# One 512-column value projection at the end of units 1 and 2, in place of two of 256 columns

## The chip, the cores and the metric

The kernel runs on one core of a Trainium2 chip. The metric is device microseconds of one execution; the figure for a kernel is the median of its runs. Times inside an execution are counted from the start of the profiler's span. TensorE is PE in the rows (its weight loads PEld), VectorE is DVE, ScalarE is ACT, and the DMA queue is SyncE's, SP.

## The reference, cut to what matters

```python
hn = rmsnorm(h_res, norm_w) * (1 + scale) + shift
proj = hn @ w_in
dq, dk, dv, dg, gq, gk, gv, gg, glr = split(proj, IN_OFFSETS)
a_out = diff_attention(rope(dq), rope(dk), dv, lam)
a_out = rmsnorm(a_out, diff_norm_w) * (1 - lam_init) * silu(dg)
b_out = gla_chunk_causal(gq, gk, gv, log_a)
b_out = rmsnorm(b_out, gla_norm_w) * silu(gg)
mixed = concat([a_out, b_out]) @ w_out
out = rmsnorm(h_res + gate * mixed, final_norm_w)
```

There are 1024 tokens of width 2048. `dv` holds the values of 8 softmax heads (128 columns each) and `gv` those of 4 gated linear heads (256 columns each). The change touches only how these two are projected for some of the heads.

## The kernel before

**Halves and units.** Tokens go in two halves of 512. In each half, four units g = 0 to 3 follow each other; unit g does the softmax heads 2g and 2g+1 and the linear head g. Everything is carried as a pair of reduced-precision parts (high and low), so each product is three matmuls. TensorE is shared by all of it, and each engine runs its own list of instructions strictly in the order that the compiler's scheduler wrote; it need not be the order of the source.

**A unit, in the order of the source** (`unit`, L821 to L885): projections `dk`, `dq`, `dg` of the first head, the narrow slab `dv` of the unit (L846), attention of the first head, `dk`, `dq`, `dg` and attention of the second, `gq`, two gate projections `gg`, the narrow slab `gv` (L873), and the linear head (`gla`, L773 to L817). The scheduler runs attention and `gla` of one unit among the projections of the same and the next unit. In unit 0 of the first half the projections were made earlier, and its linear head runs late, during unit 1.

**Two kinds of projection.** `proj_b` (L194) makes one tile of 128 features by 512 tokens: 48 matmuls with 512 columns moving. `proj_a` (L204) makes a slab with tokens on the partitions: for 256 columns 192 matmuls with 256 columns moving, 16 input blocks by 4 token blocks by 3. Its results are two PSUM tiles `pa_0` and `pa_1`, each with two token blocks.

**Weights.** Each piece is 128x1024 (`wload`, L168): one DMA into one of two raw buffers `wr`, then a high part by ScalarE (L179) and a low part by VectorE (L180) into one of three buffers `w`. A piece can be converted only when TensorE has done with the piece three before it.

**PSUM.** All projections take their tiles in turn from one pool of four banks (`pj`, L109). A tile's next user waits until the last reader of the bank has finished. At a unit's end the turn is `dg` of the second head, `gq`, first `gg`, second `gg`, and then the slab: a narrow slab takes the banks of `dg` and `gq`; a slab of four tiles would also take those of the two `gg`.

**What frees these banks.** `gq` is read by L836 and L837, which write the one buffer `gq`; they wait for the last matmul of the unit before's linear head (`o`, L804), which reads that buffer. The first `gg` bank is free after `silu_gate` has copied it (L242) into the one buffer `gg`; that copy waits until the unit before has used its `gg` up: the linear head's output is normalized, transposed by TensorE (`to`, L815), multiplied by the gate (L816), and split and stored, for j = 0 and 1, through one buffer `wr2` (`mix_out`, L731): the second split waits for the first store to land.

**Leaving PSUM.** `split` (L228) is a ScalarE cast and a VectorE subtraction from the same bank. `gv` leaves in two pairs of 128x512 (L882), `dv` in four of 128x256 (L612). In the first half the values `vb` take two of three `vb` buffers, `gv` the third and the one buffer `ka`; the buffer `va` is not used until the half's end.

**Side work.** In the first half, units 1 and 2, a list `later` (norm rows, L953, for the second half, and the first rows of the gate, L906) is spread among the weight loads: each row is a 256 KB load to a two-part buffer `stage`, one or two VectorE operations, and for the norm rows a store. At the end of unit 3, `second_hn` (L957) loads 8 pairs of input blocks back through the buffers `ka`, `va`, `kb` in turn and splits them into `hn` for the second half.

Of the kernel before, what the change touches and what calls it, by code (L numbers as in the profile page):

```python
# [10 lines left out]
F32 = mybir.dt.float32  # L11
F32R = mybir.dt.float32r
# [7 lines left out]
P = 128  # L20
# [24 lines left out]
OFF = dict(dq=0, dk=1024, dv=2048, dg=3072, gq=4096, gk=4608, gv=5120, gg=6144, glr=7168)  # L45
# [8 lines left out]
B_AT = {c: i for i, c in enumerate(B_CHUNKS)}  # L54

A_SLABS = [(n, g) for g in range(4) for n in ("dv", "gv")] + [("gk", 1)]
A_AT = {c: i for i, c in enumerate(A_SLABS)}


def lay_out(inputs):  # L60
    f = lambda a: np.ascontiguousarray(np.asarray(a))
    x = f(inputs["x"])[0]
    w = f(inputs["w_in"])[0].reshape(KT, P, -1)
    out = {}
    out["x"] = f(x)
    out["xt"] = f(x.reshape(2, TOK, KT, P).transpose(0, 3, 2, 1))
    out["ct"] = f(inputs["c"]).reshape(KT, P).T.copy()
    ada = f(inputs["w_ada"])[0].reshape(8, 2, P, 3, 8, 256)
    out["wada"] = f(ada[:, :, :, 1::-1].transpose(4, 0, 2, 1, 3, 5)).reshape(8, 8, P, 2, 512)
    out["wada0"] = f(out["wada"][0].reshape(8, P, 2, 2, 2, P).transpose(4, 0, 2, 1, 3, 5).reshape(2, 4, 4, P, 256).transpose(0, 1, 3, 2, 4))  # L70
    out["wgate"] = f(ada[:, :, :, 2].reshape(KT, P, 4, 512).transpose(2, 0, 1, 3))
    out["winb"] = f(np.stack([w[:, :, OFF[n] + i * P:OFF[n] + (i + 1) * P] for n, i in B_CHUNKS]).transpose(0, 2, 1, 3))
    out["wina"] = f(np.stack([w[:, :, OFF[n] + i * 256:OFF[n] + (i + 1) * 256] for n, i in A_SLABS]).transpose(0, 2, 1, 3))
    out["wing"] = f(np.concatenate([w[:, :, OFF["gk"]:OFF["gk"] + 256], w[:, :, OFF["glr"]:OFF["glr"] + 16]], axis=2).transpose(1, 0, 2))
    out["wout"] = f(f(inputs["w_out"])[0].reshape(KT, P, 4, 512).transpose(2, 1, 0, 3))
    out["nw"] = f(f(inputs["norm_w"])[0].reshape(KT, P).T)
    b = f(inputs["b_ada"])[0]
    out["bss"] = f(b[:2 * D].reshape(2, KT, P).transpose(2, 0, 1))
    out["bg"] = f(b[2 * D:].reshape(1, D))
    out["lam"] = f(np.stack([f(inputs[n])[0] for n in ("lambda_q1", "lambda_q2", "lambda_k1", "lambda_k2")]).reshape(1, 256))  # L80
    out["dnw"] = f(f(inputs["diff_norm_w"])[0].reshape(P, 1))
    out["gw2"] = f(inputs["gla_gate_w2"])[0].copy()
    out["gb"] = f(inputs["gla_gate_b"])[0].reshape(1, 512).copy()
    out["gnw"] = f(f(inputs["gla_norm_w"])[0].reshape(2, P).T)
    out["fw"] = f(inputs["final_norm_w"]).reshape(1, D).copy()
    inv = (np.float32(10000.0) ** (-np.arange(0, 64, 2, dtype=np.float32) / np.float32(64))).astype(np.float32)
    ang = (np.arange(S, dtype=np.float32)[None, :] * inv[:, None]).astype(np.float32)
    cos, sin = np.cos(ang).astype(np.float32), np.sin(ang).astype(np.float32)
    out["rope"] = f(np.stack([np.concatenate([cos] * 4), np.concatenate([-sin, sin, -sin, sin])], axis=1))
    j = np.arange(P)  # L90
    out["ltri"] = f(((j[:, None] // CHUNK == j[None, :] // CHUNK) & (j[:, None] > j[None, :])).astype(np.float32))
    out["ind"] = f((j[:, None] // CHUNK == np.arange(2)[None, :]).astype(np.float32))
    return out


def body(ctx, tc, A, out):
    nc = tc.nc
# [18 lines left out]
    vs_d = [dram.tile([P, 4, 2, P], F32, name=f"vsd{h}", tag=f"vsd{h}") for h in range(HEADS)]  # L116
# [70 lines left out]
    hn = [None] * KT  # L187
# [16 lines left out]
    def proj_a(src, act, n=256, kpp=4, per_bank=2):  # L204
        nb = 4 // per_bank
        pss = [pj_p.tile([P, TOK], F32, name=f"pa{w_n[0]}_{b}", tag="pj") for b in range(nb)]
        for k0 in range(0, KT, kpp):
            kn = min(kpp, KT - k0)
            w = wload(src[:, k0:k0 + kn, :], kn * n)
            for t in range(4):  # L210
                ps = pss[t // per_bank]
                o = ps[:, (t % per_bank) * n:(t % per_bank) * n + n]
                for kk in range(kn):
                    kt = k0 + kk
                    ah, al = act[kt][:, 0, t * P:(t + 1) * P], act[kt][:, 1, t * P:(t + 1) * P]
                    wh, wl = w[:, 0, kk * n:(kk + 1) * n], w[:, 1, kk * n:(kk + 1) * n]
                    st = kt == 0 and t % per_bank == 0
                    PE.matmul(o, ah, wh, start=st, stop=False, skip_group_check=True)  # L218
                    PE.matmul(o, ah, wl, start=False, stop=False, skip_group_check=True)  # L219
                    PE.matmul(o, al, wh, start=False, stop=kt == KT - 1, skip_group_check=True)  # L220
        return pss
# [6 lines left out]
    def split(hi, lo, src, lo_eng=None):  # L228
        SC.copy(hi, src)
        (lo_eng or V).tensor_tensor(lo, src, hi.bitcast(F32), ALU.subtract)  # L230
# [58 lines left out]
    for c in range(N_FIRST):  # L289
        n, i = B_CHUNKS[c]  # L290
# [149 lines left out]
    pss = st_tiles(0, 4, "b")  # L440
# [164 lines left out]
    def make_v(pss, half, g):  # L605
        vt = [hd_p.tile([P, 4, 2, P], F32R, name=f"vb{half}_{2 * g + i}", tag="vb", bufs=3) for i in range(2)]
        for b in range(2):
            v4 = pss[b].rearrange("p (t h d) -> p t h d", t=2, h=2)
            for i in range(2):
                hi, lo = vt[i][:, 2 * b:2 * b + 2, 0, :], vt[i][:, 2 * b:2 * b + 2, 1, :]  # L610
                with tc.high_priority(offset=EVAC):
                    split(hi, lo, v4[:, :, i, :])  # L612
        if half == 0:
            for i in range(2):
                nc.sync.dma_start(vs_d[2 * g + i], vt[i].bitcast(F32))
        return vt
# [200 lines left out]
            mix_out(gg[:, j, :], wr2, half, 8 + 2 * g + j)  # L817

    QS = P ** -0.5

    def unit(half, g, first, kdec):  # L821

# [20 lines left out]
        kb0 = make_k(src("dk", h0), half, h0)  # L843
        qt0 = make_q(src("dq", h0), half, h0)
        g0 = gate_tile(h0)
        vt = make_v(dv_ps if first else proj_a(A["wina"][A_AT[("dv", g)]], hn), half, g)  # L846
        attention(half, h0, qt0, kb0, vt[0], g0)
        kb1 = make_k(src("dk", h1), half, h1)
        qt1 = make_q(src("dq", h1), half, h1)
# [19 lines left out]
            tmp = misc.tile([P, 2, TOK], F32, name=f"ggt{half}{g}{j}", tag="rt", bufs=2)  # L869
            silu_gate(gg[:, j, :], s_, gnw[:, j:j + 1], tmp)  # L870
        swap = half == 0 and g == GHEADS - 1
        if not first:
            pss = proj_a(A["wina"][A_AT[("gv", g)]], hn)  # L873
        if swap:
            second_hn()
        spare_ka = half == 0 and not swap
        gv = [hd_p.tile([P, 4, 256], F32R, name=f"gv{half}{g}{i}", tag="ka" if spare_ka and i else "vb",
                        bufs=None if spare_ka and i else 3) for i in range(2)]
        for b in range(2):
            ts = slice(2 * b, 2 * b + 2)  # L880
            with tc.high_priority(offset=EVAC):
                split(gv[0][:, ts, :], gv[1][:, ts, :], gv_acc[:, ts, :] if first else pss[b].rearrange("p (t c) -> p t c", t=2))  # L882
# [225 lines left out]
```

## Time and profile before

| | us |
|---|---|
| median of 3 runs (1954.07 to 1956.4) | 1954.24 |
| the profiled execution, its own time | 1955.52 |
| its span, first to last instruction | 1953.7 |
| PE busy in the span | 1905.5 (98%) |
| DVE busy in the span | 1321.9 (68%) |
| ACT busy in the span | 968.7 (50%) |
| PE's part of the chain that ended last | 86% |

The profiled execution lies 1.3 us above the median, and its span 1.8 us below its own time. Busy time of PE runs from a matmul's start to its end, and neighbours overlap, so the step from one start to the next is what a matmul takes of the engine. Idle time is named with the instruction behind it and what released it.

In the first half the narrow slabs lie, by the timeline of PE, at 301.9 to 326.2 (`dv` of unit 1), 401.2 to 430.3 (`gv` of unit 1), 469.8 to 497.9 (`dv` of unit 2), 577.7 to 611.5 (`gv` of unit 2), 651.7 to 677.8 (`dv` of unit 3) and 753.8 to 779.2 (`gv` of unit 3).

### The profile page before, as it was taken

What the parts mean: (1) busy time and instruction counts of PE and PEld (TensorE: products, weight loads), DVE (VectorE), ACT (ScalarE), POOL (GpSimd) and SP (SyncE); (2) the same over time, 40 slices, a digit from 0 to 9 for tenths busy, and PEclk for the clock granted to TensorE, in tenths of its full rate; (3) what the DMA queues carried; (4) which work ended last, traced back from release to release, by engine and by line L of the source; (5) the groups of instructions that cost most, each with busy time, mean ns of one, the idle gap of its engine ahead of it and who ended that gap; (6) DMA issues with size and microseconds to landing.
All of it is one profiled execution on the core that took longest, in us unless ns stands there. A gap on an engine that the chain in (4) does not pass through costs nothing.

```text
span 1953.7 us, 28965 instructions
## 1 busy us (share of the span) xinstructions
PE 1905.5 (98%) x11118; PEld 1677.0 (86%) x11118; DVE 1321.9 (68%) x2496; ACT 968.7 (50%) x1811; POOL 0.7 (0%) x6
## 2 busy tenths in 40 slices
PE   7999999999989999999999999999999999899998
PEld 4888999899868989889899898989888998688888
DVE  7897876577779767656676666866785675534444
ACT  4222865566545566545545555554654544323323
POOL 0000000000000000000000000000000000000000
PEclk9899999999999999999999999999999999799999
DMA  9884434332665444433344323533263723466543
GB/s 362 294 290 136 155 125 141 119 106 87 209 210 166 136 138 150 135 89 101 97 154 117 106 91 108 162 111 99 87 198 117 267 86 106 167 239 213 162 150 120
DMA packets 111758, 298.16 MB, mean 153 GB/s; under 512 B 11098, under 2 KB 31322, under 8 KB 111108
## 3 DMA queue, kind: packets, MB, share of 16 engines
q1 hardware_dynamic: 111620, 296.32, 46.6%
q8 instruction: 87, 1.43, 0.3%
q14 instruction: 51, 0.42, 0.1%
HBM read 258.00 MB, written 38.28 MB: 152 GB/s over the span
## 4 chain that ended last, share of the span: by engine, by line
PE 86%; DMA 6%; DVE 6%; issue 1%; ACT 1%; SPq 0%; DVEq 0%; ACTq 0%
PE pa L218 8%; PE pa L220 8%; PE pa L219 8%; PE pa L1051 4%; PE pa L1052 4%; PE pa L1053 4%; PE pb_dk L190 2%; PE pb_dk L191 2%; PE pb_dk L192 2%; PE pb_gg L190 2%; PE pb_dg L191 2%; PE pb_dq L192 2%; PE pb_dq L191 2%; PE pb_dq L190 2%; PE pb_dg L192 2%; PE pb_gg L192 2%
## 5 line engine op out<-in xcount | busy, mean ns | idle before, releaser
L180 DVE TENSOR_TENSOR w<-wr,w 128x1024 fp32r<-128x1024 f32 (+1 forms) x294 | 352.1, 1198 | 276.0 <-ACT w L179 274.8
L179 ACT CAST w<-wr 128x1024 fp32r<-128x1024 f32 (+1 forms) x294 | 303.2, 1031 | 431.2 <-PE pa L1053 116.1
L220 PE MATMUL pa<-w,hn 128*128 128x256 f32 (+1 forms) x1152 | 328.2, 285 | 0.0
L218 PE MATMUL pa<-w,hn 128*128 128x256 f32 (+1 forms) x1152 | 327.7, 285 | 0.0
L219 PE MATMUL pa<-w,hn 128*128 128x256 f32 (+1 forms) x1152 | 327.7, 285 | 0.0
L219 PEld LDWEIGHTS pa<-w,hn 128*128 128x128 f32 x1152 | 219.6, 191 | 2.4 <-issue 0.2
L218 PEld LDWEIGHTS pa<-w,hn 128*128 128x128 f32 x1152 | 219.5, 191 | 2.3 <-issue 0.5
L220 PEld LDWEIGHTS pa<-w,hn 128*128 128x128 f32 x1152 | 219.5, 191 | 1.5 <-issue 0.2
L678 ACT ACTIVATE p<-s,sm 128x512 f32<-128x512 f32 (+2 forms) x192 | 110.7, 580 | 130.1 <-DVE sm L675 59.0
L1051 PE MATMUL pa<-w,mx 128*128 128x512 f32 x384 | 150.7, 392 | 0.4 <-DVE h L996 0.4
L1052 PE MATMUL pa<-w,mx 128*128 128x512 f32 x384 | 150.4, 392 | 0.0
L1053 PE MATMUL pa<-w,mx 128*128 128x512 f32 x384 | 149.9, 392 | 0.0
L669 DVE TENSOR_REDUCE sm<-s 128x1 f32<-128x512 f32 (+2 forms) x192 | 105.5, 551 | 46.7 <-PE s L666 44.1
L190 PE MATMUL pb_gg<-hn,w 128*128 128x512 f32 x224 | 88.1, 394 | 0.6 <-DVE vb L230 0.6
L191 PE MATMUL pb_dk<-hn,w 128*128 128x512 f32 x224 | 88.1, 393 | 0.0
L190 PE MATMUL pb_dk<-hn,w 128*128 128x512 f32 x224 | 88.1, 393 | 0.0
L190 PE MATMUL pb_dg<-hn,w 128*128 128x512 f32 x224 | 88.1, 393 | 0.0
L191 PE MATMUL pb_gg<-hn,w 128*128 128x512 f32 x224 | 88.0, 393 | 0.0
L192 PE MATMUL pb_dq<-hn,w 128*128 128x512 f32 x224 | 87.9, 392 | 0.0
L191 PE MATMUL pb_dg<-hn,w 128*128 128x512 f32 x224 | 87.8, 392 | 0.0
L192 PE MATMUL pb_gg<-hn,w 128*128 128x512 f32 x224 | 87.8, 392 | 0.0
L192 PE MATMUL pb_dk<-hn,w 128*128 128x512 f32 x224 | 87.6, 391 | 0.0
(394 smaller groups left out, 4376.9 us busy)
## 6 DMA issues: line engine op xcount, KB each, us to landing
wr<-in_winb SPq DMA_DIRECT2D x142, 512.0 KB, 3.8
wr<-in_wina SPq DMA_DIRECT2D x72, 512.0 KB, 3.8
wr<-in_wout SPq DMA_DIRECT2D x64, 512.0 KB, 3.5
ada<-in_wada SPq DMA_DIRECT2D x44, 512.0 KB, 5.0
stage<-in_wgate SPq DMA_DIRECT2D x64, 256.0 KB, 3.0
mx<-mixd SPq DMA_DIRECT2D x32, 512.0 KB, 8.1
ada_kdec<-in_wada SPq DMA_DIRECT2D x20, 512.0 KB, 6.6
mixd<-wr_d SPq DMA_DIRECT2D x16, 512.0 KB, 4.5
```

The source lines that it names most:

```text
L179: paced = SC.copy(w[:, 0, :n], raw[:, :n])
L180: (lo_eng or V).tensor_tensor(w[:, 1, :n], raw[:, :n], w[:, 0, :n].bitcast(F32), ALU.subtract)
L190: PE.matmul(ps, w_hi, h[:, 0, :], start=first, stop=False)
L191: PE.matmul(ps, w_hi, h[:, 1, :], start=False, stop=False)
L192: PE.matmul(ps, w_lo, h[:, 0, :], start=False, stop=last)
L218: PE.matmul(o, ah, wh, start=st, stop=False, skip_group_check=True)
L219: PE.matmul(o, ah, wl, start=False, stop=False, skip_group_check=True)
L220: PE.matmul(o, al, wh, start=False, stop=kt == KT - 1, skip_group_check=True)
L678: SC.activation(p_[:, :n], pss[pi][:, :n], AF.Exp, bias=nm, scale=0.125, accum_out=sm[:, 4 + 2 * m_ + pi:5 + 2 * m_ + pi])
L1051: PE.matmul(pss[t_], ah, wh, start=kt == 0, stop=False)
L1052: PE.matmul(pss[t_], ah, wl, start=False, stop=False)
L1053: PE.matmul(pss[t_], al, wh, start=False, stop=kt == KT - 1)
```

## The change

Units 1 and 2 of the first half end with one slab of 512 columns: the unit's own `gv` (256) and the next unit's `dv` (256), from weights laid side by side (`winw`). It takes eight pieces of two input blocks, and four PSUM tiles, one for each token block. It leaves PSUM in twelve pairs: per token block one of 128x256 (`gv`) and two of 128x128 (`dv` of each head). The next unit's values lie in the buffers `ka` and `va`, both `gv` parts in `vb`; units 2 and 3 project no `dv` of their own. Unit 0, the `dv` of unit 1, the `gv` of unit 3 and the second half are as before.

```diff
@@ -54,6 +54,8 @@
 B_AT = {c: i for i, c in enumerate(B_CHUNKS)}
 
 A_SLABS = [(n, g) for g in range(4) for n in ("dv", "gv")] + [("gk", 1)]
+
+WIDE = (1, 2)
 A_AT = {c: i for i, c in enumerate(A_SLABS)}
 
 
@@ -71,6 +73,9 @@
     out["wgate"] = f(ada[:, :, :, 2].reshape(KT, P, 4, 512).transpose(2, 0, 1, 3))
     out["winb"] = f(np.stack([w[:, :, OFF[n] + i * P:OFF[n] + (i + 1) * P] for n, i in B_CHUNKS]).transpose(0, 2, 1, 3))
     out["wina"] = f(np.stack([w[:, :, OFF[n] + i * 256:OFF[n] + (i + 1) * 256] for n, i in A_SLABS]).transpose(0, 2, 1, 3))
+    out["winw"] = f(np.stack([np.concatenate([w[:, :, OFF["gv"] + g * 256:OFF["gv"] + (g + 1) * 256],
+                                              w[:, :, OFF["dv"] + (g + 1) * 256:OFF["dv"] + (g + 2) * 256]], axis=2)
+                              for g in WIDE]).transpose(0, 2, 1, 3))
     out["wing"] = f(np.concatenate([w[:, :, OFF["gk"]:OFF["gk"] + 256], w[:, :, OFF["glr"]:OFF["glr"] + 16]], axis=2).transpose(1, 0, 2))
     out["wout"] = f(f(inputs["w_out"])[0].reshape(KT, P, 4, 512).transpose(2, 1, 0, 3))
     out["nw"] = f(f(inputs["norm_w"])[0].reshape(KT, P).T)
@@ -817,6 +822,7 @@
             mix_out(gg[:, j, :], wr2, half, 8 + 2 * g + j)
 
     QS = P ** -0.5
+    ahead = []
 
     def unit(half, g, first, kdec):
 
@@ -843,7 +849,7 @@
         kb0 = make_k(src("dk", h0), half, h0)
         qt0 = make_q(src("dq", h0), half, h0)
         g0 = gate_tile(h0)
-        vt = make_v(dv_ps if first else proj_a(A["wina"][A_AT[("dv", g)]], hn), half, g)
+        vt = ahead.pop() if ahead else make_v(dv_ps if first else proj_a(A["wina"][A_AT[("dv", g)]], hn), half, g)
         attention(half, h0, qt0, kb0, vt[0], g0)
         kb1 = make_k(src("dk", h1), half, h1)
         qt1 = make_q(src("dq", h1), half, h1)
@@ -869,14 +875,26 @@
             tmp = misc.tile([P, 2, TOK], F32, name=f"ggt{half}{g}{j}", tag="rt", bufs=2)
             silu_gate(gg[:, j, :], s_, gnw[:, j:j + 1], tmp)
         swap = half == 0 and g == GHEADS - 1
-        if not first:
+        wide = half == 0 and g in WIDE
+        if wide:
+            pss = proj_a(A["winw"][WIDE.index(g)], hn, n=512, kpp=2, per_bank=1)
+        elif not first:
             pss = proj_a(A["wina"][A_AT[("gv", g)]], hn)
         if swap:
             second_hn()
-        spare_ka = half == 0 and not swap
+        spare_ka = half == 0 and first
         gv = [hd_p.tile([P, 4, 256], F32R, name=f"gv{half}{g}{i}", tag="ka" if spare_ka and i else "vb",
                         bufs=None if spare_ka and i else 3) for i in range(2)]
-        for b in range(2):
+        if wide:
+            vt = [hd_p.tile([P, 4, 2, P], F32R, name=f"vw{2 * g + 2 + i}", tag=("ka", "va")[i]) for i in range(2)]
+            for t_ in range(4):
+                split(gv[0][:, t_, :], gv[1][:, t_, :], pss[t_][:, 0:256])
+                for i in range(2):
+                    split(vt[i][:, t_, 0, :], vt[i][:, t_, 1, :], pss[t_][:, 256 + i * P:256 + (i + 1) * P])
+            for i in range(2):
+                nc.sync.dma_start(vs_d[2 * g + 2 + i], vt[i].bitcast(F32))
+            ahead.append(vt)
+        for b in range(0 if wide else 2):
             ts = slice(2 * b, 2 * b + 2)
             with tc.high_priority(offset=EVAC):
                 split(gv[0][:, ts, :], gv[1][:, ts, :], gv_acc[:, ts, :] if first else pss[b].rearrange("p (t c) -> p t c", t=2))
```

The scheduler writes new lists for all engines from unit 1's end on. Three places follow.

**ScalarE, end of unit 1.** `wrg` are the two splits of unit 0's linear output, `gg` the two copies that free the banks `pb_gg`, `qt` the queries of head 3. Before:

```order
L678 ACTIVATE p_3439,sm_3432<-s_3433,sm_3432 128x384
L229 CAST wrg_2901<-gg_acc 128x512
L179 CAST w_4511<-wr_4509 128x1024
L678 ACTIVATE p_3447,sm_3432<-s_3441,sm_3432 128x384
L242 COPY gg_3966<-pb_gg_3967 128x512
L229 CAST aT_3422<-tp_3418 128x384
L229 CAST gv_4346<-pa_0_4107 128x512
L240 ACTIVATE ggt_4098<-pb_gg_4037 128x512
L242 COPY gg_3966<-pb_gg_4037 128x512
```

The change:

```order
L683 ACTIVATE p_3447,sm_3432<-s_3441,sm_3432 128x384
L234 CAST wrg_2901<-gg_acc 128x512
L697 ACTIVATE p_3447<-p_3447,sm_3432 128x384
L605 CAST qt_3_3670<-rt_q_3662 64x512
L606 CAST qt_3_3670<-rt_q_3662 64x512
L605 CAST qt_3_3670<-rt_q_3662 64x512
L606 CAST qt_3_3670<-rt_q_3662 64x512
L234 CAST aT_3422<-tp_3418 128x384
L247 COPY gg_3966<-pb_gg_3967 128x512
L683 ACTIVATE p_3461,sm_3454<-s_3455,sm_3454 128x512
L245 ACTIVATE ggt_4098<-pb_gg_4037 128x512
L247 COPY gg_3966<-pb_gg_4037 128x512
```

Between the second split `wrg` and the first copy `gg` stood one weight conversion and one exponential; now a scaling, four casts of `qt` and one of `aT` stand there, and the weight conversions have moved behind both copies.

**TensorE, end of unit 1.** `to` are the transposes of unit 0's linear output, `s`, `tp`, `av` belong to attention. Before:

```order
L815 MATMUL to_2902<-ident,yg_2801 128x128
L815 MATMUL to_2911<-ident,yg_2801 128x128
L219 MATMUL pa_1_4108<-w_4185,hn_660 128x256
L815 MATMUL to_2902<-ident,yg_2801 128x128
L815 MATMUL to_2911<-ident,yg_2801 128x128
L220 MATMUL pa_1_4108<-w_4185,hn_660 128x256
L218 MATMUL pa_1_4108<-w_4185,hn_664 128x256
L219 MATMUL pa_1_4108<-w_4185,hn_664 128x256
L220 MATMUL pa_1_4108<-w_4185,hn_664 128x256
```

The change, where `pa_2` is the slab's third tile and its first three weight pieces have by then been used for `pa_0` and `pa_1`:

```order
L820 MATMUL to_2911<-ident,yg_2801 128x128
L670 MATMUL s_3433<-kb_2_2989,qt_2_3064 128x384
L671 MATMUL s_3433<-kb_2_2989,q_lo 128x384
L713 MATMUL tp_3418<-ident,p_3380 128x128
L670 MATMUL s_3441<-kb_2_2989,qt_2_3064 128x384
L671 MATMUL s_3441<-kb_2_2989,q_lo 128x384
L670 MATMUL s_3455<-kb_2_2989,qt_2_3064 128x512
L671 MATMUL s_3455<-kb_2_2989,q_lo 128x512
L670 MATMUL s_3463<-kb_2_2989,qt_2_3064 128x512
L671 MATMUL s_3463<-kb_2_2989,q_lo 128x512
L713 MATMUL tp_3418<-ident,p_3402 128x128 x2
L725 MATMUL av_3417<-aT_3422,vb_2_3360 128x256
L223 MATMUL pa_2_4109<-w_4113,hn_298 128x512
```

Before, the slab went on between and behind the transposes; now nothing of the slab stands between them and the first matmul into `pa_2`, only ten attention instructions in a row of waits.

**SyncE's queue, end of unit 3.** `xtb` are the loads of `second_hn`; `hnd_136` is its second, through the buffer `va`. Before it stood among unit 2's loads:

```order
L177 DMA wr_5474<-in_winb 128x1024
L951 DMA hnd_136<-stage 128x512 x2
L895 DMA stage<-in_xt 128x512 x2
L963 DMA xtb_7428<-hnd_136 128x1024
L177 DMA wr_5507<-in_winb 128x1024
```

The change:

```order
L182 DMA wr_7256<-in_winb 128x1024
L981 DMA xtb_7084<-hnd_138 128x1024
L182 DMA wr_7287<-in_winb 128x1024
L981 DMA xtb_7068<-hnd_136 128x1024
L182 DMA wr_7333<-in_winb 128x1024
L981 DMA xtb_7108<-hnd_141 128x1024
L981 DMA xtb_7092<-hnd_139 128x1024
L182 DMA wr_7362<-in_winb 128x1024
```

It now stands behind the first two weight pieces of the second half.

## Rows read from the trace of the kernel before

**Rows 1.** The page, engines: busy us, share of the span, instructions.

```profile
PE 1905.5 (98%) x11118; PEld 1677.0 (86%) x11118; DVE 1321.9 (68%) x2496; ACT 968.7 (50%) x1811; POOL 0.7 (0%) x6
```

**Rows 2.** Windows: stretch, length, busy us of PE, PEld, DVE, ACT, POOL; clock; DMA.

```profile
401.20:430.20 29.00, 29.00 (x234) 28.51 (x234) 22.12 (x64) 18.01 (x40) 0.00 (x0) 1.00 0.35 114
430.20:545.90 115.70, 115.70 (x645) 100.89 (x644) 87.34 (x175) 67.28 (x124) 0.00 (x0) 1.00 0.46 145
545.90:611.40 65.50, 56.97 (x357) 49.05 (x356) 52.55 (x132) 30.54 (x66) 0.00 (x0) 1.00 0.66 202
611.40:779.00 167.60, 167.60 (x983) 148.08 (x982) 127.72 (x257) 101.61 (x189) 0.00 (x0) 1.00 0.43 141
...
753.80:779.20 25.40, 25.40 (x211) 25.29 (x210) 20.91 (x31) 17.07 (x30) 0.00 (x0) 1.00 0.46 151
```

**Rows 3.** Timeline of PE in a narrow slab: start us, length us, instruction; 27 steps apart.

```profile
582.64 0.28 PE L219 MATMUL pa<-w,hn 128*128 128x256 f32 x1
...
585.87 0.28 PE L219 MATMUL pa<-w,hn 128*128 128x256 f32 x1
```

**Rows 4.** Timeline of PE in the output projection, 512 columns; 70 steps apart.

```profile
1700.02 0.39 PE L1051 MATMUL pa<-w,mx 128*128 128x512 f32 x1
...
1715.88 0.39 PE L1052 MATMUL pa<-w,mx 128*128 128x512 f32 x1
```

**Rows 5.** Groups by form: count | busy us, mean ns | idle before, releaser.

```profile
L229 ACT CAST vb<-pa 128x256 fp32r<-128x256 f32 x28 | 9.9, 373 | 12.8 <-PE pa L220 6.9 <-DVE vb L230 5.8
L229 ACT CAST gv<-pa 128x512 fp32r<-128x512 f32 x14 | 8.2, 587 | 3.5 <-PE pa L220 3.5
L230 DVE TENSOR_TENSOR vb<-pa,vb 128x256 fp32r<-128x256 f32 x28 | 11.3, 417 | 5.9 <-ACT vb L229 5.8
L230 DVE TENSOR_TENSOR gv<-pa,gv 128x512 fp32r<-128x512 f32 x14 | 9.3, 680 | 2.2 <-PE av L722 2.2
```

**Rows 6.** Timeline of PE, unit 1's narrow gv slab.

```profile
401.25 0.28 PE L218 MATMUL pa<-w,hn 128*128 128x256 f32 x1
...
409.08 0.64 PE L804 MATMUL o<-sr,gq 128*128 128x512 f32 x2
...
416.68 0.38 PE L815 MATMUL to<-ident,yg 128*128 128x128 f32 x2
```

**Rows 7.** Timeline of ACT in the same stretch; in brackets idle before and its releaser.

```profile
418.68 0.62 ACT L229 CAST wrg<-gg_acc 128x512 fp32r<-128x512 f32 x1 [1.43 <-DVE gg_acc L816]
...
423.51 0.62 ACT L229 CAST wrg<-gg_acc 128x512 fp32r<-128x512 f32 x1 [1.42 <-DMA mixd<-wrg]
424.04 1.05 ACT L179 CAST w<-wr 128x1024 fp32r<-128x1024 f32 x1
...
425.55 0.57 ACT L242 COPY gg<-pb_gg 128x512 f32<-128x512 f32 x1
...
428.36 0.62 ACT L600 CAST qt<-rt_q 64x512 fp32r<-64x512 f32 x1
```

**Rows 8.** Waits of PE, 545 to 612 us: us in total, times, longest.

```profile
PE s L665 <- ACT p L678: 4.6, 5, 1.9
PE tp L708 <- DVE s L668: 2.7, 1, 2.7
```

**Rows 9.** Windows again: two thin stretches of PE and what followed the second.

```profile
578.00:581.00 3.00, 0.45 (x4) 0.24 (x2) 2.79 (x6) 2.65 (x5) 0.00 (x0) 1.00 0.57 126
1661.00:1666.00 5.00, 2.25 (x7) 1.96 (x8) 2.25 (x5) 0.99 (x2) 0.00 (x0) 0.58 0.48 157
1676.00:1681.00 5.00, 4.36 (x9) 3.01 (x10) 3.71 (x8) 1.81 (x6) 0.00 (x0) 0.50 0.58 182
1681.00:1686.00 5.00, 5.00 (x21) 4.07 (x20) 4.27 (x13) 1.77 (x6) 0.00 (x0) 0.87 1.03 390
```

**Rows 10.** SP's queue: one store's issue; loads issued 740:800, KB each, us to landing.

```profile
420.06 0.33 SPq L733 DMA_DIRECT2D mixd<-wrg  x1
...
xtb<-hnd SPq DMA_DIRECT2D x4, 512.0 KB, 5.1
```

## The prediction

> **What bounds the kernel now.** I read the engine totals first, then the windows at the places of the change, then PE's, ScalarE's and SP's timelines at unit 1's end. PE is busy 98% of the span, VectorE 68%, ScalarE 50% [rows 1]. So a microsecond of PE work taken away or added counts in full where PE is never idle, and an idle one counts in full too. In the windows the reader is to compare PE's busy time with the length: from 401.2 to 545.9 and from 611.4 to 779.0 they are equal; only unit 2's end (545.9 to 611.4) shows 56.97 busy of 65.5, 8.5 us idle [rows 2]. Its named waits are scores behind an exponential of ScalarE (4.6 us) and transposes behind VectorE's copy of scores (2.7 us) [rows 8], in a stretch where VectorE is busy 52.55 us [rows 2]. The first half therefore has almost no slack on PE: what the change saves in matmuls comes off, and any new wait goes on top.
>
> **The matmuls: −4.8 us.** Four narrow slabs of 192 matmuls go. A step is (585.87 − 582.64)/27 = 119.6 ns [rows 3], so 768 × 0.1196 = 91.9 us. Two wide slabs of 192 come. In the output projection a 512-column step is (1715.88 − 1700.02)/70 = 226.6 ns [rows 4], so 384 × 0.2266 = 87.0 us. The gain is 4.8 us: about 13 ns less than twice the narrow step, 384 times. The Trainium skill ("TensorE: Matmul & The Clock Gate", section "Wait — 56ns, not 53.3ns?") gives a warm matmul N/2.4 GHz plus about 2.5 ns; by that 256 columns take 109 ns and 512 take 216, and the gain would be only 1.0 us. Both steps measured here are longer and their fixed part is larger, so I go by the rows.
>
> **The weights: 0.** Each slab of 256 columns took four pieces, the wide one takes eight: the same loads, the same casts and subtractions. They lie beside PE's work. If that cover went, a piece would cost its ScalarE cast of 1.05 us [rows 7] at most.
>
> **Unit 1's third tile: +11 us, the main term.** The narrow slab used the banks of `dg` and `gq`; the wide one's third tile needs the first `gg` bank, so its first matmul waits for ScalarE's copy of it. That copy waits for unit 0's linear head, whose chain is in the rows. Its last output matmul begins at 409.08, its last transposes at 416.68 [rows 6]; the first split of its result is at 418.68, the store is issued at 420.06 [rows 10], the second split starts at 423.51 after idling 1.42 us for that store to land, and the copy begins at 425.55 [rows 7]. Before, nobody on PE waited for this.
> - When the copy ends now. ScalarE's new list has, from the second split to the copy, the split, a scaling, four casts of `qt` and one of `aT`: seven operations, each no longer than about the 0.62 us of such a cast [rows 7], 4.3 us. With the copy of 0.57, from 423.51 to 428.4. The chain itself starts earlier: ahead of the last output matmul stand 18 slab matmuls (4.1 us), six others of 256 columns (0.7), all six outputs (1.4) and four short scores (0.3), so it ends at 407.7 instead of 409.7, 2 us sooner. How much of that the splits keep the rows don't show: 0 if they wait for other work of their engines, 3 if a weight cast of 1.05 us [rows 7] that stood ahead of them goes too. So the copy ends between 425.4 and 428.4; I take 426, near the 2 us that are worked out.
> - When PE is there. From 401.25 [rows 6] until the third tile PE has 36 matmuls of the slab, 8.2 us, and 42 others with 11,392 columns together. A step is 12.6 ns plus 0.418 ns a column [rows 3, 4], so these are 5.3 us. It has run out at 414.75.
> - The wait is 426 − 414.75 = 11 us; bounds 10.6 and 13.7. It may be spread over the scores, transposes and the `av` that stand just before the third tile, as they wait for ScalarE's list too. Behind it are queued the fourth tile, the rest of head 3's attention, and the fourth weight piece, whose cast has moved behind both copies; PE holds all three `w` buffers until the third and fourth tiles have used them. Those tiles give 36 × 0.2266 = 8.2 us of work meanwhile, so the late cast costs nothing more.
>
> **The clock: +2 us.** PE has some 2 us of work in those 11. In two thin stretches of this kernel the granted clock was 1.00 (PE busy 0.45 of 3 us) and 0.58, then 0.50, with 0.87 in the 5 us after [rows 9]. At half clock 5 us hold 2.5 us of work, so the price lies between 0 and 2.8 us. I take 2: the longer thin stretches are the nearer rows.
>
> **Leaving PSUM: +1 us.** Per wide slab, 12 casts and 12 subtractions replace 6 and 6. By the 256- and 512-column forms [rows 5] a ScalarE cast of 128 columns is about 0.27 us, VectorE's 0.285; ScalarE gets 4 × 0.373 + 8 × 0.27 = 3.6 us for 2 × 0.587 + 4 × 0.373 = 2.7, VectorE 3.9 for 3.0. Both engines have room. But the next unit's `dk` takes the first tile's bank: that tile's last matmul is 18 × 0.2266 = 4.1 us before the slab's end, and its three pairs take 0.37 + 0.42 + 2 × (0.27 + 0.285) and some 0.2 us at each of five handovers, 2.9 us, mixed with the second tile's. It is just free in time; I take 0.5 us per slab. Without this cover it could be 5 each: bounds 0 and 10.
>
> **Unit 2's end: 0.** The 8.5 us of idle time come with side rows on VectorE, and these are as many as before; scores still queue behind them. There the linear head of unit 1 runs earlier, so that its `gg` banks are not late. Bounds −8.5 (all gone) and +6 (a wait of half unit 1's).
>
> **The halves' border: +3 us.** The buffer `va` now holds head 7's values, so the second, fifth and eighth loads of `second_hn` go through it late and one after the other. The second stands behind two weight pieces of the second half; a piece goes out when the slab is five pieces behind it (three `w`, two `wr` buffers), that is 5 × 25.4/8 = 16 us after the slab of 25.4 us [rows 2] begins, plus a cast of 1.05: at +17. Each load takes 5.1 us to land [rows 10] and two casts and a subtraction of the 512-column size, 0.59 + 0.59 + 0.68 [rows 5]: 7 us. So the three are ready at +24, +31 and +38. `dk` begins at +25.4 and needs them after 6, 24 and 42 matmuls of 0.2266 us: at +26.8, +30.8 and +34.9. The last is 3 us late; bounds 0 (VectorE and ScalarE overlap with the next load) and 6.
>
> **Sum.** −4.8 + 11 + 2 + 1 + 0 + 3 = +12.2 us. The profiled execution took 1955.5; the change gives 1967.7. The median of the runs shown is 1.3 below that execution, so I predict 1966.4. With the main terms' own bounds the forecast reaches from 1960 to 1973.
>
> **Rivals.**
> - *Paid back in unit 2.* VectorE has 52.55 us of work in 65.5 [rows 2], and the 4 us of `dv` splits leave unit 2's start for unit 1's wait. If the scores there come ahead of the side rows, up to 8.5 us of idle time go, and the sum is +3.7: 1957.9, not slower by what can be measured; with no clock loss 1956. It decides if the wait of 2.7 us behind the score copy [rows 8] is gone. Against it: the rows' number is the same and PE, less loaded, asks sooner.
> - *No wait in unit 1.* If the copy ended before 414.75, PE would find its bank; 13 us go and it is −0.8: 1953.4, or 1949.4 if the ends cost 0. For it, only that the chain may be tightened by its order; against it, that the second split was at 423.51 and would have to come 9 us sooner.
> - *Late ends.* If splitting in smaller pieces holds the next `dk` by 5 us per slab, it is 9 more: 1975.4. For it speaks the tight sum above; against it ScalarE's 50%.
> - *No gain from width.* If the wide step is twice the narrow one, 239 ns, the 4.8 us are not there: 1971.2. For it speaks nothing in the rows: 226.6 is measured with the same operand types [rows 4].
>
> **Chances.** Forecast 0.50, paid back 0.20, no wait 0.10, late ends 0.15, no gain from width 0.05. About 0.2% (3.9 us) is what a measurement of this kernel can tell from no change: faster is below 1950.3, slower above 1958.1. Slower: the forecast, late ends, no gain, less a little for smaller costs together, 0.68. Same: most of paid back and half of no wait, 0.21. Faster: the other half, and paid back with a short wait, 0.11. The range is 1949 to 1980: it takes in both low rivals almost wholly and the late ends to half of their bounds, and leaves out below 2 in 10.
>
> **What would show it.** In the changed profile: steps of 226 ns in the slab; PE idle some 11 us between 414 and 427, released by ScalarE, at or shortly before the third tile; a granted clock under 1 just behind it; PE idle again 8 us at unit 2's end; the next `dk` beginning within a microsecond of each wide slab's end; a wait of some 3 us for the normalized input in the second half's first `dk`. The forecast is wrong if PE is busy through 414 to 427, or if unit 2's end has no idle time, or if a wait of over 5 us stands anywhere else.

## The result and the profile after

The change takes 1965.22 us (median of 4 runs, 1961.87 to 1966.51); the kernel before, 1954.93 in the same series. The ratio is 1.0051, with a 95% interval of 1.0037 to 1.0064: slower by about 10 us. The prediction was 1966.4 in a range of 1949 to 1980, with 0.68 on slower. The profiled execution took 1966.51 us, its span 1964.7.

The span is counted from the first to the last instruction. The engine totals of the change (columns as in [rows 1]):

```profile
PE 1909.1 (97%) x10734; PEld 1661.1 (85%) x10734; DVE 1322.1 (67%) x2508; ACT 969.2 (49%) x1823; POOL 0.7 (0%) x6
```

PE has 384 instructions less than before and yet 3.6 us more of busy time. That alone says that matmuls took longer somewhere. The windows say where. First the whole stretch in which the change can act, from the first matmul of unit 1's last slab to the first `dk` of the second half, before and then after (length, busy us of PE, PEld, DVE, ACT, POOL; clock; DMA):

```profile
401.20:779.00 377.80, 369.27 (x2211) 326.53 (x2211) 289.74 (x624) 217.44 (x416) 0.00 (x0) 1.00 0.47 151
```

```profile
403.30:787.70 384.40, 370.64 (x1828) 309.32 (x1827) 288.35 (x632) 216.65 (x425) 0.00 (x0) 0.98 0.46 148
```

It is 6.6 us longer. PE's idle time went from 8.5 to 13.8 us, and its busy time rose from 369.3 to 370.6 us at a mean clock below 1. Divided into unit 1's slab, unit 2's projections up to `dg`, unit 2's end with its slab, and unit 3 (they answer to [rows 2]):

```profile
403.30:471.80 68.50, 62.18 (x294) 50.76 (x293) 51.34 (x148) 41.23 (x93) 0.00 (x0) 0.93 0.27 87
471.80:549.00 77.20, 76.15 (x356) 62.76 (x355) 59.83 (x112) 41.97 (x77) 0.00 (x0) 1.00 0.56 180
549.00:648.10 99.10, 92.71 (x428) 74.92 (x427) 73.29 (x158) 47.15 (x93) 0.00 (x0) 0.98 0.54 170
648.10:787.70 139.60, 139.60 (x757) 120.89 (x756) 103.90 (x217) 86.30 (x164) 0.00 (x0) 1.00 0.45 144
```

Unit 1's slab has 6.3 us of idle time where there was none; unit 2 has 1.1 and 6.4, together 7.4, where there were 8.5 [rows 2]; unit 3 has none, before and after. The place in unit 1, in PE's timeline (in brackets the idle time ahead and its releaser):

```profile
409.20 0.90 PE L809 MATMUL o<-sr,gq 128*128 128x512 f32 x3
411.52 0.51 PE L223 MATMUL pa<-w,hn 128*128 128x512 f32 x1 [1.41 <-DVE gq L843]
...
416.25 1.04 PE L820 MATMUL to<-ident,yg 128*128 128x128 f32 x8
417.71 0.44 PE L670 MATMUL s<-kb,qt 128*128 128x384 f32 x1 [0.43 <-ACT p L683]
...
419.54 0.44 PE L670 MATMUL s<-kb,qt 128*128 128x384 f32 x1 [1.10 <-ACT p L683]
...
421.24 0.80 PE L670 MATMUL s<-kb,qt 128*128 128x512 f32 x1 [1.01 <-ACT p L683]
...
426.22 0.58 PE L725 MATMUL av<-aT,vb 128*128 128x256 f32 x1 [2.37 <-ACT aT L234]
426.70 0.79 PE L223 MATMUL pa<-w,hn 128*128 128x512 f32 x1
```

The last output matmuls of unit 0's linear head begin at 409.20, the transposes at 416.25, and the third tile's first matmul at 426.70. In [rows 6] the last transposes began at 416.68 and the slab simply went on. Between the transposes and the third tile there are now only attention's matmuls (twelve, not ten as counted ahead of the prediction), with four waits among them of 0.43, 1.10, 1.01 and 2.37 us. ScalarE in the same stretch:

```profile
417.94 0.62 ACT L234 CAST wrg<-gg_acc 128x512 fp32r<-128x512 f32 x1 [0.28 <-DVE gg_acc L821]
...
422.24 0.62 ACT L234 CAST wrg<-gg_acc 128x512 fp32r<-128x512 f32 x1
422.77 0.61 ACT L697 ACTIVATE p<-p,sm 128x384 f32<-128x384 f32 x1
423.28 0.60 ACT L605 CAST qt<-rt_q 64x512 fp32r<-64x512 f32 x1
...
425.70 0.47 ACT L234 CAST aT<-tp 128x384 fp32r<-128x384 f32 x1
426.07 0.58 ACT L247 COPY gg<-pb_gg 128x512 f32<-128x512 f32 x1
```

The first split of the linear output is at 417.94, the second at 422.24, then a scaling, four query casts (the first is shown) and `aT`, and the copy of the first `gg` from 426.07 for 0.58 us. It ends at 426.65, and the third tile begins at 426.70. That is the bank that the prediction named, and the order in which it said the work would stand. The granted clock in and behind that stretch, and behind unit 2's longest wait:

```profile
415.00:420.00 5.00, 3.47 (x22) 2.61 (x20) 3.78 (x13) 2.08 (x6) 0.00 (x0) 0.99 0.01 2
420.00:425.00 5.00, 2.84 (x7) 1.45 (x6) 4.27 (x19) 4.35 (x10) 0.00 (x0) 0.50 0.28 116
425.00:430.00 5.00, 3.78 (x9) 2.92 (x10) 3.68 (x10) 4.95 (x12) 0.00 (x0) 0.50 0.23 94
430.00:435.00 5.00, 5.00 (x30) 4.35 (x29) 3.85 (x10) 2.06 (x6) 0.00 (x0) 0.98 0.00 0
560.00:563.00 3.00, 0.86 (x4) 0.69 (x5) 2.73 (x7) 2.97 (x7) 0.00 (x0) 1.00 0.61 184
563.00:567.00 4.00, 4.00 (x12) 3.12 (x11) 3.89 (x8) 0.71 (x2) 0.00 (x0) 0.57 0.58 219
```

It was 0.50 from 420 to 430, and 0.57 in 563 to 567, where PE was busy all the time. Half clock on 2.84 and 3.78 us of busy time costs 1.4 and 1.9 us; with the edges and with 4.0 x 0.43 = 1.7 in unit 2 it is 5.2 us for the half. So 365.4 us of the 370.6 are full-clock work, 3.8 less than the 369.3 of before, and -3.8 + 5.3 of idle time + 5.2 of clock is the 6.6 (with rounding).

The other 4.4 us of the 11.0 by which the spans differ lie in code that the change leaves alone: unit 1's last slab began 2.1 us later, and the stretch behind the half is 2.3 us longer. In the twelve profiles of this study that slab begins between 400.7 and 406.2 us: latest (404.5 and above) in the three with fewer side rows, in the other nine in no order with the width of the slabs. The stretch behind the half lasts 1171.9 to 1177.0 us; the change has the longest, and the kernel with unit 2 alone wide the shortest. How much of the 10 us of the medians is such scatter and how much follows from the change further back isn't settled.

### The profile page after: what moved, and what is told of

The parts are those of the page before. It is cut to its first block, busy times and chain, and to the rows that moved or that the text cites. A ratio compares the mean times of both kernels' runs of the same rounds, so it can differ in the third digit from the quotient of the medians.

```text
span 1964.7 us, 28228 instructions
## 1 busy us (share of the span) xinstructions
PE 1909.1 (97%) x10734; PEld 1661.1 (85%) x10734; DVE 1322.1 (67%) x2508; ACT 969.2 (49%) x1823; POOL 0.7 (0%) x6
## 4 chain that ended last, share of the span: by engine, by line
PE 84%; DMA 7%; DVE 6%; issue 1%; ACT 1%; SPq 0%; DVEq 0%; ACTq 0%
PE pa L223 8%; PE pa L225 8%; PE pa L224 8%; PE pa L1069 4%; PE pa L1071 4%; PE pa L1070 4%; PE pb_gg L195 2%; PE pb_dk L196 2%; PE pb_dk L195 2%; PE pb_dk L197 2%; PE pb_gg L197 2%; PE pb_gg L196 2%; PE pb_dq L197 2%; PE pb_dq L196 2%; PE pb_dq L195 2%; PE pb_dg L196 2%
## 5 line engine op out<-in xcount | busy, mean ns | idle before, releaser
L223 PE MATMUL pa<-w,hn 128*128 128x256 f32 (+2 forms) x1024 | 307.1, 301 | 1.4 <-DVE gq L843 1.4
L224 PE MATMUL pa<-w,hn 128*128 128x256 f32 (+2 forms) x1024 | 306.6, 300 | 0.0
L225 PE MATMUL pa<-w,hn 128*128 128x256 f32 (+2 forms) x1024 | 306.5, 300 | 0.0
L223 PEld LDWEIGHTS pa<-w,hn 128*128 128x128 f32 x1024 | 195.6, 191 | 8.7 <-DVE gq L843 1.8
L224 PEld LDWEIGHTS pa<-w,hn 128*128 128x128 f32 x1024 | 196.0, 191 | 6.5 <-issue 0.2
L225 PEld LDWEIGHTS pa<-w,hn 128*128 128x128 f32 x1024 | 195.8, 191 | 6.4 <-issue 0.2
L195 PE MATMUL pb_dg<-hn,w 128*128 128x512 f32 x224 | 88.2, 394 | 0.0
L195 PE MATMUL pb_dq<-hn,w 128*128 128x512 f32 x224 | 88.1, 393 | 0.0
L197 PE MATMUL pb_dq<-hn,w 128*128 128x512 f32 x224 | 87.8, 392 | 0.0
```

Source lines behind the costliest of these rows:

```text
L195: PE.matmul(ps, w_hi, h[:, 0, :], start=first, stop=False)
L197: PE.matmul(ps, w_lo, h[:, 0, :], start=False, stop=last)
```

## Experiments

The kernel before ran beside each, and ratios are to it. Where a text says `va`, `kb` or `vb`, these are the 4 KB buffers of keys and values.

### One unit at a time

```diff
-WIDE = (1, 2)
+WIDE = (1,)
...
-        spare_ka = half == 0 and first
+        spare_ka = half == 0 and not swap and not wide
```

> Only unit 1 ends with the wide slab; unit 2 and the values of unit 3 are narrow as before. Theory (the loss is unit 1's wait for the first gg bank, some 10 us with the half clock behind it): -2.4 us of matmuls plus 10, about 1962 (1959 to 1965), with PE idle some 6 us between 410 and 427 and a clock near 0.5 behind it. Rival (the loss is spread: both units, the splits in smaller pieces, the half's border): half of the change's +10, about 1959 or less, and no long wait in unit 1.

1966.1 us, ratio 1.0061 (1.0047 to 1.0074): more than the 1959 to 1965 that were expected. PE's waits inside the slab are those of the full change: 2.5 us for exponentials, 2.4 for `aT`, 1.4 for `gq`. Its first half, from unit 1's slab, is 9.4 us longer than before:

```profile
402.70:789.90 387.20, 373.83 (x2019) 319.90 (x2018) 290.73 (x630) 217.48 (x422) 0.00 (x0) 0.98 0.46 147
```

The other unit, with `WIDE = (2,)` and the same line for `spare_ka`:

> Only unit 2 ends with the wide slab; unit 1 and the values of unit 2 are narrow as before. Theory: unit 2's gg banks are free in time, so only the matmuls change: -2.4 us, about 1952.5 (1950 to 1955), not slower than before. Rival (a wide slab costs in either unit, by its splits and by the later loads at the half's border): 1957 to 1960.

1950.48 us, ratio 0.9976 (0.9966 to 0.9985): faster than before. Its first half, from the narrow slab of unit 1:

```profile
403.70:776.50 372.80, 366.80 (x2020) 316.03 (x2019) 289.98 (x628) 217.42 (x421) 0.00 (x0) 1.00 0.48 152
```

PE's busy time is 369.27 - 366.80 = 2.5 us less, as the step sizes said for one unit, and its idle time 6.0 instead of 8.5; the clock is full throughout. So unit 1 carries the whole loss, and a wide slab in unit 2 costs nothing. Whether the two add up can't be told from the medians: unit 1 alone loses 11.2 us and unit 2 alone gains 4.4, against the 10.3 lost by both, and each of these intervals reaches 2 to 3 us either way. By the profiled halves, a wide unit 2 beside a wide unit 1 takes off 387.2 - 384.4 = 2.8 us, close to the matmuls of one unit, and alone 377.8 - 372.8 = 5.0. In both kernels with unit 1 wide, PE waits 2.5 to 2.7 us in one go for attention's `p` in unit 2 and a half clock follows (0.57 from 563 to 567 in both); with unit 2 alone the longest wait is 2.1 us and the clock stays full. Why isn't shown.

### The banks of gg

The first copy goes to `va`, and the last step of the gate reads it there and writes `gg`:

```diff
-            SC.copy(dst, src)
+            SC.copy(mid, src)
...
-        V.scalar_tensor_tensor(dst, dst, neg_w, d, ALU.mult, ALU.mult)
+        V.scalar_tensor_tensor(dst, mid, neg_w, d, ALU.mult, ALU.mult)
...
+        via = hd_p.tile([P, 2, TOK], F32, name="ggv", tag="va") if half == 0 and g == 1 else None
```

> The change, but unit 1's gg is copied from its banks into the buffer va, free until the slab ends, and multiplied from there into gg: the first copy no longer waits for unit 0's linear head. The second copy still stands late in ScalarE's list, behind the queries' casts, so the fourth tile waits as before. Theory (the banks are the wait): the third tile's 18 matmuls (4.1 us) and their neighbours fill part of the hole, 5 of 10 us stay: about 1960 (1956 to 1963). Rival (PE waits for attention's scores and transposes, which ScalarE serves late, whatever the banks): 1964 to 1967, no gain.

1962.06 us, ratio 1.0036 (1.0022 to 1.005): 3 us of the loss are gone, where 5 were expected, within the range of 1956 to 1963. The third tile's matmuls moved ahead of the hole; the fourth stayed behind it, and the hole with its half clock (5.5 us idle) came a few microseconds later. Next, both banks: `gg` itself in `va`, the second head's values in `gg`.

```diff
-        gg = gg_acc if first else gla_p.tile([P, 2, TOK], F32, name=f"gg{half}{g}", tag="gg")
+        gg = gg_acc if first else (hd_p if wide else gla_p).tile([P, 2, TOK], F32, name=f"gg{half}{g}", tag="va" if wide else "gg")
...
-            vt = [hd_p.tile([P, 4, 2, P], F32R, name=f"vw{2 * g + 2 + i}", tag=("ka", "va")[i]) for i in range(2)]
+            vt = [(gla_p if i else hd_p).tile([P, 4, 2, P], F32R, name=f"vw{2 * g + 2 + i}", tag=("ka", "gg")[i]) for i in range(2)]
```

> The change, but units 1 and 2 keep their gg in the buffer va, and the second head's values ahead lie in the buffer gg instead: no operation more or less, and neither copy of gg in unit 1 waits for unit 0's linear head, so all four banks are free when the slab begins. Theory (the banks are the wait): PE is busy through 403 to 430 at full clock, and what is left is the matmuls' gain: about 1951 (1948 to 1955), faster than before. Rival (attention's chain on ScalarE is the wait): PE still idles 5 us or more there, 1960 or more. If the time lies between, the new place of the values costs elsewhere (unit 3's gg then waits for head 7's values).

1955.32 us, ratio 1.0006 (0.9997 to 1.0014). The hole is gone, as the theory of the banks said, but the time is still not below before and lies just above the expected 1948 to 1955. The windows of unit 1's slab (its halves, then from its last matmul to the next `dk`, then behind that):

```profile
402.10:430.00 27.90, 27.90 (x136) 23.52 (x135) 19.07 (x51) 14.84 (x33) 0.00 (x0) 1.00 0.32 99
430.00:453.90 23.90, 23.90 (x118) 19.91 (x116) 15.99 (x45) 14.91 (x33) 0.00 (x0) 1.00 0.36 111
453.90:463.60 9.70, 6.39 (x29) 4.25 (x28) 8.48 (x31) 6.95 (x22) 0.00 (x0) 0.86 0.31 108
463.60:468.00 4.40, 4.40 (x12) 3.41 (x11) 4.40 (x15) 2.91 (x6) 0.00 (x0) 0.54 0.31 126
```

PE is busy from 402.1 to 453.9 at full clock, with the same scores and transposes in between that it had waited for: they were never the limit while there was slab work to do. But `dk` begins 9.7 us after the slab's last matmul, PE is idle for 3.3 of these, and the clock falls to 0.54 behind. In PE's timeline (the last slab matmul, the end of head 2's `av`, the first `dk`):

```profile
453.56 0.39 PE L225 MATMUL pa<-w,hn 128*128 128x512 f32 x1
...
458.28 0.27 PE L727 MATMUL av<-aT,vb 128*128 128x128 f32 x1
...
463.63 0.63 PE L195 MATMUL pb_dk<-hn,w 128*128 128x512 f32 x1
```

and VectorE right behind that `av`:

```profile
458.59 1.42 DVE L235 TENSOR_TENSOR gv<-pa,gv 128x256 fp32r<-128x256 f32 x4
```

The four low parts of `gv` are written only when head 2's values have been read for the last time: they share the three `vb` buffers. Until then no tile of the slab can leave PSUM, and `dk` needs a bank. `dk` itself begins 3.6 us after these four, behind more of attention's matmuls in PE's list; whether the buffer is the cause, the next edit tells.

### The buffer behind the banks

```diff
-        gv = [... tag="ka" if spare_ka and i else "vb", ...]
+        gv = [... tag="kb" if (wide and g == 1) and i else "ka" if spare_ka and i else "vb", ...]
```

> As the kernel with gg in va, but unit 1's low part of gv lies in one of the two key buffers kb instead of a vb buffer, which head 2's values hold until their attention ends. Theory (behind the banks of gg stands a second wait: the slab's tiles can't leave PSUM until head 2's values are read, so the next dk begins 9.7 us after the slab's last matmul): the next dk begins within 2 us of the slab, the half-clock stretch there goes, and the time is that kernel's 1955.3 less 5 to 8, about 1949 (1947 to 1952). Rival (the tail of attention itself holds PE at the slab's end, whatever the buffers): 1953 to 1956.

1951.66 us, ratio 0.9982 (0.9973 to 0.999): faster than before, and 3.7 us faster than its parent where 5 to 8 were expected. The slab's last matmul and the first `dk`:

```profile
455.57 0.39 PE L225 MATMUL pa<-w,hn 128*128 128x512 f32 x1
...
456.75 0.47 PE L195 MATMUL pb_dk<-hn,w 128*128 128x512 f32 x1
```

1.2 us apart instead of 10, with no wait. And its first half:

```profile
404.10:776.60 372.50, 365.17 (x1828) 306.78 (x1827) 288.86 (x633) 217.19 (x427) 0.00 (x0) 1.00 0.48 153
```

Clock 1.00, 365.17 us of work: the matmuls' whole gain is 369.3 - 365.2 = 4.1 us. The hole at the slab's end is closed in full. What is missing of the expected gain is in step with the idle time of unit 2: 7.3 us here, 4.9 in the kernel before it.

The same for unit 2's `gv` (`wide and i`):

> The same for unit 2's low part of gv too. Unit 2's slab was followed by the next dk after 0.6 us already, so the theory expects nothing more: within 1 us of the kernel before it, about 1949. Rival (unit 2's slab also waits for value buffers, hidden in its idle time): 2 us or more faster than that.

1950.61 us, ratio 0.998 (0.9972 to 0.9989): no difference to the kernel before it that these intervals can tell, as expected.

### Another way around the banks

```diff
-            pss = proj_a(A["winw"][WIDE.index(g)], hn, n=512, kpp=2, per_bank=1)
+            passes = ((0, 1), (2, 3)) if g in TWO else ((0, 1, 2, 3),)
+            pss = []
+            for blocks in passes:
+                pss += proj_a(A["winw"][WIDE.index(g)], hn, n=512, kpp=2, per_bank=1, blocks=blocks)
```

with `TWO = (1,)`, so that two tiles are made at a time.

> The change, but unit 1's slab goes in two passes of two tiles (token blocks 0 and 1, then 2 and 3), each with all eight weight pieces loaded anew: the first pass uses the banks of dg and gq alone, the second begins some 25 us later, when both copies of gg are done. Eight more weight pieces, 1.05 us of ScalarE and 1.2 of VectorE each, beside PE. Theory of the banks: no hole between 410 and 427, about 1955 to 1958, as the value buffers still hold the slab's end. Rival (ScalarE's and VectorE's lists are the limit, so eight more pieces make it worse): 1966 or more.

1961.74 us, ratio 1.0032 (1.002 to 1.0044): between the two expectations. Its windows in unit 1, the last one from the slab's last matmul to `dk`:

```profile
400.70:430.00 29.30, 27.89 (x136) 23.06 (x135) 23.04 (x60) 17.40 (x37) 0.00 (x0) 1.00 0.46 144
...
457.70:469.40 11.70, 6.29 (x19) 4.23 (x20) 10.64 (x35) 8.12 (x26) 0.00 (x0) 0.65 0.49 173
```

The hole of 410 to 427 shrank to 1.4 us, as the banks say. But the stretch at the slab's end is 11.7 us long here, 5.4 of them idle, with the clock at 0.65, and VectorE writes the low parts of `gv` only behind head 2's last `av` again. So this version takes away the first wait and meets the second in full. It is 4 us slower than the theory allowed; VectorE is busy 10.64 of those 11.7 us, the extra weight pieces among it, so the rival (the two engines' lists are the limit) may have a share, which no run separates.

### Unit 2's idle time

One side row after every third weight piece, `PACE = 3` instead of 2, on three kernels: the one with both low parts in `kb`, the kernel before, and the one with unit 2 alone.

> As the kernel with both low parts of gv in kb, and one side row after every third weight piece instead of every second, so that the norm rows reach into unit 3. Theory (the 6 to 8 us that PE still idles in unit 2 come with the side rows' work on VectorE): PE's idle time in the first half falls from 6.5 us to about 3, and the time by as much, to about 1947 (1944 to 1950). Rival (the idle time is attention's own chain of scores, exponentials and transposes): no change, 1950 to 1952; or the rows are now late for the second half: 1955 or more.

> The kernel before, with a side row after every third weight piece: the control of the run before this one. Theory: its 8.5 us of idle time in unit 2 fall to about 4, 1950.5 (1948 to 1953). Rival (attention's own chain): no change, 1954 to 1956.

> Only unit 2 wide, with a side row after every third weight piece. By the theory 1950.5 less some 2 to 3 of its 6.0 us of idle time: about 1948 (1946 to 1950). Rival: no change, 1949.5 to 1951.5.

They took 1949.41 us (ratio 0.9969, 0.9956 to 0.9981), 1950.91 (0.9977, 0.9969 to 0.9986) and 1950.2 (0.9977, 0.9966 to 0.9988). The control is the telling one, the kernel before with its rows thinned out, by the window of its first half and its only wait there:

```profile
404.50:775.30 370.80, 366.24 (x2198) 326.84 (x2197) 288.62 (x617) 217.54 (x420) 0.00 (x0) 1.00 0.49 157
```

```profile
PE to L815 <- DVE yg L810: 4.6, 1, 4.6
```

Idle time fell from 8.5 to 4.6 us. Unit 2 has none left; the 4.6 are a single new wait in unit 3 (transposes for VectorE), with half clock behind it. So the side rows did cause unit 2's idle time. The first of the three has the lowest median of the study, 5.4 us under before, with 5.0 us of idle time where about 3 were expected. The third missed its 1946 to 1950 and gained nothing over unit 2 alone; its `dk` now waits 3.5 us for VectorE's splits of the slab. Thinning the rows alone, one number and no wide slab, gained 3.9 us, and the intervals of all three overlap: that wide slabs gain anything beside thinned rows isn't shown.

## Why the prediction was right

The sign and the main mechanism held: the third tile's bank, the chain that frees it, and the half clock. The size held in part by luck: the terms summed to +12.2 us, and what they stand for measured +6.6. The total came near only with 4.4 us of the spans from stretches for which the prediction had no term.

- **Matmuls, -4.8 us.** Right in kind (91.9 - 87.0 is 4.9, a slip of no weight). In the wide slab (23 steps between the first two rows, and the next `dk` in the last):

```profile
465.31 0.39 PE L223 MATMUL pa<-w,hn 128*128 128x512 f32 x1
...
470.53 0.40 PE L225 MATMUL pa<-w,hn 128*128 128x512 f32 x1
470.76 0.49 PE L713 MATMUL tp<-ident,p 128*128 128x128 f32 x3
471.01 0.96 PE L793 MATMUL kv<-gv,kd_z 128*128 128x256 f32 x6
471.81 0.39 PE L195 MATMUL pb_dk<-hn,w 128*128 128x512 f32 x1
```

  (470.53 - 465.31)/23 = 227 ns, as in [rows 4]. The work fell by 2.5 us for one unit and by 4.1 for two, at full clock. By the Trainium skill ("TensorE: Matmul & The Clock Gate", section "Wait — 56ns, not 53.3ns?") the gain for two is an estimated 1.0 us; the measurement differs and decides, for a larger fixed part of a matmul.
- **Unit 1's third tile, +11, and the clock, +2.** The third tile came 23.4 us after the slab's start, for which 13.5 us of work were counted: 9.9 us late. That the copy ended at 426.65, where 426 was taken, is luck in part: the slab began 2.05 us later than before. Counted from its start the copy ended at 23.35, below the taken 24.75 and the lower bound of 24.15. The chain had run sooner than allowed for: the second split came 18.9 us after the slab's start, and 22.3 before [rows 6, 7]. The shares were off too. Idle are 6.3 us, 1.4 of them earlier than expected, as the second tile waited at 411.52 for VectorE to empty the bank of `gq`, which the prediction hadn't seen. Half clock is 3.4 us, in the thin stretch and behind it, and a second such stretch arose in unit 2 (1.7 us): 5.2 in all, so the term of +2 was mis-sized. About 1.7 us of the half clock lie ahead of the third tile; some 2 us of the 9.9 are neither, so the work took longer than counted by steps (the eight transposes 1.04 us, 0.53 by the steps).
- **Leaving PSUM, +1.** The forms measured are as estimated:

```profile
L234 ACT CAST gv<-pa 128x256 fp32r<-128x256 f32 x8 | 2.9, 368 | 1.3 <-PE pa L225 1.3
L234 ACT CAST vw<-pa 128x128 fp32r<-128x128 f32 x16 | 4.1, 268 | 3.9 <-DVE vw L235 2.2 <-DVE gv L235 1.6
L235 DVE TENSOR_TENSOR gv<-pa,gv 128x256 fp32r<-128x256 f32 x8 | 3.3, 418 | 0.6 <-ACT gv L234 0.5
L235 DVE TENSOR_TENSOR vw<-pa,vw 128x128 fp32r<-128x128 f32 x16 | 4.4, 284 | 0.9 <-ACT vw L234 0.7
```

  268 and 284 ns for 128 columns, against 0.27 and 0.285. The next `dk` begins at 471.81, directly behind the `kv` matmuls: 0 us. In the change head 2's attention is done by then, as the hole held the slab back; once the hole was closed, `dk` came 9.7 us late at this very place (3.3 of them idle, and 3.7 gained when it was mended), by another resource than the one that the bound of 5 us had in mind.
- **Unit 2's end, 0.** -1.1 us of idle time and 1.7 of half clock, within the bounds.
- **The halves' border, +3.** Wrong. The step that failed is that a piece goes out "five pieces" behind the slab, worked out with a slab of eight; unit 3's slab is narrow and has four. SP's queue (the second weight piece of the second half, and the second and last load of `second_hn` through `va`):

```profile
772.08 0.33 SPq L182 DMA_DIRECT2D wr<-in_winb  x1
773.97 0.33 SPq L981 DMA_DIRECT2D xtb<-hnd  x1
...
789.25 0.32 SPq L981 DMA_DIRECT2D xtb<-hnd  x1
```

  The second load went out 11.8 us after the slab's start at 762.2, not 17, and the last one's splits on VectorE:

```profile
793.50 1.29 DVE L235 TENSOR_TENSOR hn<-xtb,hn 128x512 fp32r<-128x512 f32 x2
```

  ended 32.6 us after it, not 38. `dk` began at 787.7 with no wait; the term is 0.

By terms: -3.8 + 6.3 + 5.2 + 0 - 1.1 + 0 = +6.6 in the half (-4.8 + 11 + 2 + 1 + 0 + 3 = +12.2 was predicted); the rest of the measured 10 lies outside of it. Of the rivals, "no gain from width" is refuted by the steps, "no wait in unit 1" by the timeline, "late ends" by 471.81, and "paid back in unit 2" by the 7.4 us that stayed. The sign that was named for this last one did come: the wait of 2.7 us behind the score copy [rows 8] is nearly gone. But another behind VectorE stands in its place (PE's waits from 545 to 650 in the change):

```profile
PE tp L713 <- DVE p L698: 3.2, 2, 2.5
...
PE tp L713 <- DVE s L673: 0.6, 1, 0.6
```

So that sign couldn't decide between the two. Side rows on VectorE do make the idle time of unit 2, as the thinned-out rows show; the change doesn't thin them.

## What to carry to other kernels

A wider tile saves a fixed amount per matmul, and it takes more PSUM banks and result buffers at once: for each of them look up who has it then, and follow that holder's whole chain, through stores and through the other work in its engine's list. Freeing the first such resource only showed the second (`dk` 9.7 us behind the slab); it took both to keep 3 to 4 us, while using the wide form only where the holders are done early gained 4.4 us with two lines, and thinning the side rows of the old kernel 3.9 us with one number. And a wait that names attention may be a symptom: PE waited for scores because nothing else was allowed to run, and the same chain cost nothing once the slab could.

## What the runs showed of the hardware

The price of a hole in PE's work was not only its idle time. From 420 to 430 PE was busy 6.6 of 10 us at a granted clock of 0.50, and in 563 to 567 the clock was 0.57 with PE busy throughout, behind a stretch of 3 us with 0.86 us of work. The kernel before had holes of 8.5 us in all in the same half, one stretch of 0.45 busy in 3 us among them [rows 9], and its clock stayed at 1.00. So 13.8 us of holes cost 5.2 us of clock in one kernel, and 8.5 cost none in the other. Their sum alone doesn't decide: the kernel with `gg` in `va` had 8.2 us of holes, and its clock was 0.54 from 463.6 to 468.0. The control with thinned-out rows had 4.6 us of holes, all in one go, and behind them the granted clock was 0.50:

```profile
664.50:666.50 2.00, 2.00 (x12) 2.00 (x11) 1.16 (x3) 0.00 (x0) 0.00 (x0) 0.50 0.64 200
```
